# Splitting the weights of the attention pairs three chunks ahead, and moving the scores and their exchange, in a two-layer attention and mLSTM kernel

## The chip, the cores and the metric

The kernel runs on one core of one Trainium2 chip. The time of a run is the device time of one execution in microseconds (us). Three runs of the kernel before took 1404.33, 1407.17 and 1409.06 us; the median is 1407.17 us. Beside the times there is a profile of one execution. Its engines are TensorE (PE, with PEld for its weight loads), VectorE (DVE), ScalarE (ACT), GpSimd (POOL) and SyncE (SP), which only issues transfers here.

## The reference

Two layers over 512 tokens of width 1024, in fp32. Layer 0 has a mixer of dilated attention, layer 1 a chunkwise mLSTM; each is followed by a SwiGLU network of inner width 2816, and all have RMS norms and residual sums. The change concerns the attention, which is, cut to what matters:

```python
DIL_CONFIGS = ((128, 1), (512, 4), (2048, 16))      # window, dilation: three groups
def dilated_attention_mixer(xn, positions, w_in, w_out):
    proj = (xn @ w_in).reshape(B, S, 3, 3, 8, 128)   # group, q/k/v, head, head width
    for g, (window, dilation) in enumerate(DIL_CONFIGS):
        q = apply_partial_rope(proj[:, :, g, 0], positions) * 128 ** -0.5
        k = apply_partial_rope(proj[:, :, g, 1], positions)
        v = proj[:, :, g, 2]
        o, lse = dilated_window_attention(q, k, v, window, dilation)
        outs.append(o); lses.append(lse)
    wts = jax.nn.softmax(jnp.stack(lses), axis=0)
    o = jnp.einsum('gbsh,gbshd->bshd', wts, jnp.stack(outs))
    return o.reshape(B, S, 1024) @ w_out
```

The rope turns only the first 32 of a head's 128 values. The weights of the groups come from the groups' softmax sums, so that all scores of a head are wanted before its probabilities can be weighed and applied to the values.

## The kernel before

**Products.** To keep fp32 accuracy on TensorE each operand is held as a high and a low part, and a product is three matmuls (high-high, high-low, low-high; `SPLITS`). A weight chunk of 128 x 1024 is loaded by SP (`load_chunk`, three places, tag "wraw"); ScalarE copies it to the high part (L210, tile names ending in _h) and VectorE subtracts to get the low part (L211, names in _l). High and low parts have three places each (tags "whi", "wlo", `W_BUFS` = 3). A split into a place has to wait until TensorE has read the chunk that lay there before.

**Pairs.** The eight heads are worked in four pairs, a0 to a3. For each pair there are q and k of three groups. Group 0 is a plain product: two chunks for q and two for k (`project`, L241, names a1g0q, a1g0k), each chunk 48 / 2 = 24 matmuls of 512 columns, for the two heads m = 0 and 1. Groups 1 and 2 are done by `qk_unit` (L904) as seven products of combined blocks, in the order P1, P5, P2, P6, P7, P3, P4 of 24 matmuls of 256 columns. Blocks of weights are combined by VectorE (`less`, L834) and then split as above (names a1g1P_h, a1g2P_l). The products go to three accumulators in PSUM (names ending in c, u, p; tag "acc", three banks). After some products ScalarE copies an accumulator out: L867 after P1, L870 after P5, L872 after P6 (whose copy P7 waits for, since it goes on in the same bank), L861 and L879 after P2 and P4; VectorE combines the parts of k (L885). The rope's steps are on VectorE (L585 to L594), and its copies back on ScalarE (L600 for group 0, eight copies; L602 for the others).

**Attention of a pair.** While TensorE does the projections of pair n, the attention of pair n - 1 is woven in. Its steps are: scores of group 0 (L678 on PE; eight masked reductions L684 on DVE; eight exponentials L715 on ACT), scores of groups 1 and 2 (L698; L701; sixteen exponentials L721), the exchange of maxima and sums and the groups' weights (`joint`, L734 on PE, small steps to L758), weighing of the first and second head (`weigh`, L766 and L769 on DVE), transposes (L775 on DVE, then four transfers of POOL to memory, L778), `bring` (L783, a transfer of POOL back), and the values (L793 and L798 on PE, names a0o). Scores use the PSUM banks of tag "s" for the first head and "o" for the second, two each; the values use "o" too. Probabilities and transposes have the tag "p" with three places, what is brought back has "pt" with two.

**What sets the order.** A chunk or a product ends with a tick (`advance`). Steps are put off by a number of ticks (`defer`): `SCORES0_AT`, `RUN_AT` (scores of groups 1 and 2; the five steps of the rest; the values; the loads of v) and `LAST_AT` for the last pair. The matmuls of such steps are kept at their place on PE by `run` and `fenced`. Weights are split by a plan: `Feed` hands out a chunk and then prepares as many as its `ahead` says (2). Beyond that a scheduler at build time decides the order on every engine; on the chip each engine goes through its own list in that order.

Of the kernel before, what the change touches and what calls it, by code (L numbers as in the profile page):

```python
# [11 lines left out]
F32 = mybir.dt.float32  # L12
# [5 lines left out]
P = 128  # L18
# [3 lines left out]
KC = D // P  # L22
TB = SEQ // P
HEADS = 8
D_FF = 2816
# [8 lines left out]
C3 = float(np.float32(TWO_PI - C1 - C2))  # L34
SCORES0_AT = 4
RUN_AT = (2, (4, 5, 6, 7, 8), (10, 11), (2, 3, 1))
LAST_AT = (1, (3, 3, 3, 3, 3), (), (1, 1, 1))
# [35 lines left out]
def tile_hybrid_dilated_attn_mlstm(  # L73
# [21 lines left out]
    nc.sync.dma_start(cst[:, :K_MT], consts[:, :K_MT])  # L95
    attn_rows = cp.tile([KC, P], F32, name="attn_rows")
    nc.gpsimd.dma_start(attn_rows, attn_norm.rearrange("a (r p) -> (a r) p", p=P))
    ones = cp.tile([P, 1], F32, name="ones")
# [42 lines left out]
    def defer(n, fn):  # L141
        later.append((tick[0] + n, next(order), fn))
# [21 lines left out]
    def last_on_pe():  # L164
        return last_on(mybir.EngineType.PE)
# [32 lines left out]
    def load_chunk(src, shape, name):  # L198
# [4 lines left out]
        return raw, n, view, name  # L203

    def split_chunk(chunk):

        raw, n, view, name = chunk
        hi = wp.tile([P, 1024], F32R, tag="whi", name=name + "_h", bufs=W_BUFS)
        lo = wp.tile([P, 1024], F32R, tag="wlo", name=name + "_l", bufs=W_BUFS)
        nc.scalar.activation(hi[:, :n], raw[:, :n], AF.Copy)  # L210
        nc.vector.tensor_tensor(lo[:, :n], raw[:, :n], hi[:, :n].bitcast(F32), op=ALU.subtract)  # L211
        return view(hi), view(lo)
# [32 lines left out]

    def project(pairs, w2d, c0, nk, evac, name, hook=None, ready=()):

        acc = [acc_tile("%s_%d" % (name, m)) for m in range(2)]
        for ch in range((nk + 3) // 4):
            n = min(4, nk - 4 * ch)  # L250
            whl = ready.pop(0) if ready else split_chunk(weight_chunk(w2d, ch, c0, n, "%s_k%d" % (name, ch)))
            for m in range(2):
                with fenced():
                    multiply(acc[m], whl, pairs, ch, m, nk)
                if 4 * ch + n == nk and hook is None:
                    evac(m, acc[m])
            if 4 * ch + n == nk and hook is not None:
                hook()
                for m in range(2):
                    evac(m, acc[m])  # L260
            advance()
# [122 lines left out]
    with ExitStack() as actx:  # L384
# [54 lines left out]


        xtok = ap.tile([P, TB, D], F32, tag="heads", name="x_tok")
        raws = [wp.tile([P, 1024], F32, tag="wraw", name="first%d_w" % i, bufs=W_BUFS) for i in range(2)]
# [189 lines left out]
        def attention_pair(pr, qks):  # L632
# [33 lines left out]
            def score_bank(i, name):  # L666
                return ps.tile([P, 512], F32, tag="so"[i], name=name, bufs=2)
# [23 lines left out]
            def scores12(qk1, qk2):  # L691

                for i in range(2):
                    for g, (q, k) in ((1, qk1), (2, qk2)):
                        sp = score_bank(i, "%ss%d" % (nm, g))
                        for c in range(4):
                            sl = slice(c * P, (c + 1) * P)
                            nc.tensor.matmul(sp[:, sl], q[:, i, sl], k[:, i, sl], start=True, stop=True)  # L698
                        for c in range(4):
                            sl = slice(c * P, (c + 1) * P)  # L700
                            nc.vector.tensor_tensor_reduce(  # L701
                                p12[i][:, 4 * (g - 1) + c, :], sp[:, sl], mask_causal if g == 1 else mask_dil,
                                1.0, -3e38, op0=ALU.add, op1=ALU.max, accum_out=mx[:, g - 1, i, c:c + 1])
                    exponentials(1, i)

# [65 lines left out]
            def transposes(i):  # L771


                t = ap2.tile([P, 4, 15, R], F32, tag="p", name=nm + "pB", bufs=3)
                nc.vector.transpose(t.rearrange("p b n i -> p n b i"), p[i])  # L775
                d = pts[i] = dp.tile([4, R, 4, 15 * R], F32, tag="d", name=nm + "pD", bufs=2)
                for a in range(4):
                    nc.gpsimd.dma_start(d.rearrange("b j a x -> a j b x")[a],  # L778
                                        t[R * a:R * (a + 1)].rearrange("p b n i -> p b (n i)"))

            def bring(i, queue=nc.gpsimd):
                pt = ap2.tile([P, 4, 15, R], F32, tag="pt", name=nm + "pT", bufs=2)
                queue.dma_start(pt.rearrange("p a n i -> p (a n i)"), pts[i].rearrange("b j a x -> (b j) (a x)"))  # L783
                pts[i] = pt
# [67 lines left out]
        def qk_unit(pr, g, qk):  # L852
# [38 lines left out]
            for n, name in enumerate(ORDER):  # L891
# [16 lines left out]
                if n == 6 and not last:  # L908
                    defer(1, rope(qk, rot, False))
                if n in (1, 3, 5, 6):  # L910
                    advance()

        def project_pair(pr, qks, then=None):
            nm = "a%d" % pr
            for g in range(3):
# [14 lines left out]
                for part in range(2):  # L930
# [58 lines left out]

        HALF = SEQ // 2  # L990
        S = {}
# [302 lines left out]


    HALF = SEQ // 2

# [1021 lines left out]
```

## Time and profile before

| what | value |
|---|---|
| runs | 1404.33, 1407.17, 1409.06 us |
| profiled execution | 1408.34 us, span 1406.6 us |
| TensorE busy | 1375.8 us |
| VectorE busy | 1104.5 us |
| ScalarE busy | 802.5 us |
| GpSimd busy | 163.8 us |
| mean granted clock of TensorE | 0.994 |

The span is the time from the first to the last instruction of the profiled execution; the execution's own time is 1.7 us longer. A row of the waits says which line of which engine waited, for whom, how long in total, how often, and the longest. A row of a timeline has the start, the duration, engine, line, operation, the tile written and those read; brackets at its end give the idle time before it and what ended it. Names have their buffer numbers left out, so that a1g2P_h is the high part of any product of group 2 of pair 1. The attention of the pairs 0 to 2 lies beside the projections of the pairs 1 to 3, between about 177 and 430 us; the last pair's attention follows.

### The profile page before, as it was taken

The page shows a single profiled execution, that of the slowest core. Times are in us where ns is not written, and L with a number is a line of the kernel's source. Part 1 is how long each engine was busy: PE and PEld are TensorE (multiplying, and loading weights), DVE is VectorE, ACT ScalarE, POOL GpSimd, SP SyncE. Part 2 cuts the span into 40 slices and gives each one's busy share as a digit, 9 for nine tenths or more (in the row PEclk, how much of TensorE's full clock was granted, in tenths as well). Part 3 has the DMA queues.
Part 4 walks back from the last instruction along what each step waited for, and adds up shares of the span by engine and source line. Part 5 has one row for each costly group of instructions (what it writes and reads, how often), then busy time and mean ns, then how long its engine had stood idle before and what let it go on. Part 6 is the DMA issues. An engine that isn't in the chain of part 4 may idle for free. (4 is left out here: it accounts for less than half of the span.)

```text
span 1406.6 us, 22635 instructions
## 1 busy us (share of the span) xinstructions
PE 1375.8 (98%) x8740; PEld 1248.3 (89%) x8740; DVE 1104.5 (79%) x1841; ACT 802.5 (57%) x1346; POOL 163.8 (12%) x238
## 2 busy tenths in 40 slices
PE   9999998999989999999999999999999999999997
PEld 7888888988888788999999998888888899999886
DVE  7768668485777289878878888988858987887887
ACT  6556566565755155544466554786534544448854
POOL 3000011111010101000000101113101240001213
PEclk9999999999999999999999999999999999999999
DMA  9534245546165546432354652333333563335963
GB/s 293 171 120 135 93 133 181 171 138 196 49 225 181 187 125 162 133 121 72 109 167 93 146 151 70 97 91 98 98 120 108 127 209 121 119 95 137 197 163 106
DMA packets 140003, 193.67 MB, mean 138 GB/s; under 512 B 8948, under 2 KB 104756, under 8 KB 139896
## 3 DMA queue, kind: packets, MB, share of 16 engines
q1 hardware_dynamic: 119552, 139.81, 31.3%
q0 software_dynamic: 18688, 51.30, 15.6%
q8 instruction: 68, 1.11, 0.3%
q10 hardware_dynamic: 1656, 1.12, 0.2%
q14 instruction: 39, 0.32, 0.1%
HBM read 167.30 MB, written 22.54 MB: 135 GB/s over the span
## 5 line engine op out<-in xcount | busy, mean ns | idle before, releaser
L1622 POOL DMA_DIRECT2D f1T<-in_ffn_w_out_dram x15 | 17.8, 1185 | 208.3 <-DMA f1P_2w_w<-in_ffn_w_out_dram 136.1
L1597 POOL DMA_DIRECT2D f0S<-in_ffn_w_out_dram x10 | 8.7, 890 | 259.5 <-DVE f0hid L1514 173.4
L2154 POOL DMA_DIRECT2D hD<-hB x32 | 21.7, 697 | 67.2 <-DVE hB L2151 67.2
L241 PE MATMUL mo<-n_h,mo_k_l 128*128 128x512 f32 x64 | 25.3, 396 | 0.0
L241 PE MATMUL mo<-n_h,mo_k_h 128*128 128x512 f32 x64 | 25.2, 394 | 0.0
L241 PE MATMUL mo<-n_l,mo_k_h 128*128 128x512 f32 x64 | 25.2, 394 | 0.0
L241 PE MATMUL mwo<-yo_l,mwo_k_h 128*128 128x512 f32 x64 | 25.1, 393 | 0.0
L241 PE MATMUL mqk<-n_h,mqk_k_h 128*128 128x512 f32 x64 | 25.1, 393 | 0.0
L241 PE MATMUL mqk<-n_l,mqk_k_h 128*128 128x512 f32 x64 | 25.1, 392 | 0.0
L241 PE MATMUL awo<-ao_h,awo_k_h 128*128 128x512 f32 x64 | 25.1, 392 | 0.0
L241 PE MATMUL f0j<-n_h,f0j_h 128*128 128x512 f32 x64 | 25.0, 391 | 0.0
L241 PE MATMUL f1j<-n_h,f1j_h 128*128 128x512 f32 x64 | 25.0, 391 | 0.0
L241 PE MATMUL mwo<-yo_h,mwo_k_l 128*128 128x512 f32 x64 | 25.0, 391 | 0.0
L241 PE MATMUL mqk<-n_h,mqk_k_l 128*128 128x512 f32 x64 | 25.0, 391 | 0.0
L241 PE MATMUL f0j<-n_h,f0j_l 128*128 128x512 f32 x64 | 24.9, 390 | 0.0
L241 PE MATMUL f1j<-n_h,f1j_l 128*128 128x512 f32 x64 | 24.9, 390 | 0.0
L241 PE MATMUL awo<-ao_h,awo_k_l 128*128 128x512 f32 x64 | 24.9, 390 | 0.0
L241 PE MATMUL awo<-ao_l,awo_k_h 128*128 128x512 f32 x64 | 24.9, 389 | 0.0
L241 PE MATMUL f0j<-n_l,f0j_h 128*128 128x512 f32 x64 | 24.9, 389 | 0.0
L241 PE MATMUL f1j<-n_l,f1j_h 128*128 128x512 f32 x64 | 24.9, 389 | 0.0
L241 PE MATMUL mwo<-yo_h,mwo_k_h 128*128 128x512 f32 x64 | 24.8, 391 | 0.0
L211 DVE TENSOR_TENSOR v1P_l<-v1W,v1P_h 128x1024 fp32r<-128x1024 f32 x14 | 17.1, 1224 | 9.3 <-ACT v1P_h L210 9.3
(2615 smaller groups left out, 5899.1 us busy)
## 6 DMA issues: line engine op xcount, KB each, us to landing
f0j_w<-in_ffn_w_in_dram SPq DMA_DIRECT2D x17, 512.0 KB, 5.3
f1j_w<-in_ffn_w_in_dram SPq DMA_DIRECT2D x17, 512.0 KB, 6.0
f1T<-in_ffn_w_out_dram POOLq DMA_DIRECT2D x15, 512.0 KB, 6.5
f0hid<-in_ffn_w_in_dram SPq DMA_DIRECT2D x9, 512.0 KB, 5.1
f1hid<-in_ffn_w_in_dram SPq DMA_DIRECT2D x9, 512.0 KB, 5.0
v0W<-in_attn_w_in_dram SPq DMA_DIRECT2D x8, 512.0 KB, 5.8
v1W<-in_attn_w_in_dram SPq DMA_DIRECT2D x8, 512.0 KB, 4.1
awo_k_w<-in_attn_w_out_dram SPq DMA_DIRECT2D x8, 512.0 KB, 4.9
```

The costliest lines, as they stand in the source:

```text
L211: nc.vector.tensor_tensor(lo[:, :n], raw[:, :n], hi[:, :n].bitcast(F32), op=ALU.subtract)
L241: nc.tensor.matmul(acc, whl[a][:, k, m * P:(m + 1) * P], pairs[b][kk], start=(kk == 0 and (a, b) == SPLITS[0]), stop=(kk == nk - 1 and (a, ...
L1597: nc.gpsimd.dma_start(t, src[1][:, ks], accum_op=ALU.add)
L1622: nc.gpsimd.dma_start(view(to), weight_rows(hk * UNITS + u, n), accum_op=ALU.add)
L2154: nc.gpsimd.dma_start(hD[k // 4].rearrange("(b i) x -> i b x", i=R)[:, :, c0:c0 + R], t[R * a_:R * (a_ + 1)])
```

## The change

The line numbers after are 3 to 15 higher in this part (L678 becomes L686, L684 L692, L715 L726, L793 L804, L798 L809, L904 L915, L210 L213, L211 L214).

- The plan prepares three chunks ahead (`feed.ahead = 3`) from the end of the values of all heads until the output projection, and every fourth split goes to a fourth place for high and low part in another pool. The raw weights keep their three places.
- `SCORES0_AT` goes from 4 to 5, so that the scores of group 0 stand one tick later, and `RUN_AT[0]` from 2 to 1: the scores of groups 1 and 2 stand after the first chunk of g0q of the next pair and no longer after the second. All their matmuls come first, then the reductions by head.
- With `amid`, steps that are due at the next tick (exchange, joint, first weighing) run within the last chunk of g0k, between its two heads, 12 matmuls sooner.
- Probabilities, transposes and what is brought back share one tag with four places (before: three and two). The first `bring` stands after the second transposes, so that on POOL's queue eight transfers to memory come ahead of both transfers back.
- The rope's copies of group 2 follow its steps at once and are not put off by a tick.
- The rope's tables are filled by half as wide copies on POOL and one transfer more for each table, and a few tiles lie in other pools.

```diff
-SCORES0_AT = 4
-RUN_AT = (2, (4, 5, 6, 7, 8), (10, 11), (2, 3, 1))
+SCORES0_AT = 5
+RUN_AT = (1, (4, 5, 6, 7, 8), (10, 11), (2, 3, 1))
...
+    spare = []
+    splits = itertools.count()
+
     def split_chunk(chunk):
         raw, n, view, name = chunk
-        hi = wp.tile([P, 1024], F32R, tag="whi", name=name + "_h", bufs=W_BUFS)
-        lo = wp.tile([P, 1024], F32R, tag="wlo", name=name + "_l", bufs=W_BUFS)
+        p, more, bufs = (spare[0], "4", 1) if spare and next(splits) % (W_BUFS + 1) == W_BUFS else (wp, "", W_BUFS)
+        hi = p.tile([P, 1024], F32R, tag="whi" + more, name=name + "_h", bufs=bufs)
+        lo = p.tile([P, 1024], F32R, tag="wlo" + more, name=name + "_l", bufs=bufs)
...
                 if 4 * ch + n == nk and hook is None:
                     evac(m, acc[m])
+                if amid and (ch, m) == (1, 0):
+                    with tc.issue_after(last_on_pe()):
+                        run_deferred(lambda t: t <= tick[0] + 1)
...
-                    nc.gpsimd.tensor_copy(
-                        to[R * (c // 2):R * (c // 2 + 1)].rearrange("p (m s) -> p m s", m=2)[:, :, c % 2 * P:(c % 2 + 1) * P],
-                        t[R * c:R * (c + 1)].unsqueeze(1).to_broadcast([R, 2, P]))
+                    nc.gpsimd.tensor_copy(to[R * (c // 2):R * (c // 2 + 1), c % 2 * P:(c % 2 + 1) * P],
+                                          t[R * c:R * (c + 1)])
+                nc.gpsimd.dma_start(to[:2 * R, HALF:], to[:2 * R, :HALF])
                 nc.gpsimd.dma_start(to[2 * R:], to[:2 * R])
...
-                p.extend(ap2.tile([P, 15, P], F32, tag="p", name="%sp%d" % (nm, i), bufs=3) for i in range(2))
+                p.extend(ap2.tile([P, 15, P], F32, tag="p", name="%sp%d" % (nm, i), bufs=4) for i in range(2))
...
-                for i in range(2):
-                    for g, (q, k) in ((1, qk1), (2, qk2)):
-                        sp = score_bank(i, "%ss%d" % (nm, g))
+                banks_ = {}
+                for g, (q, k) in ((1, qk1), (2, qk2)):
+                    for i in range(2):
+                        sp = banks_[g, i] = score_bank(i, "%ss%d" % (nm, g))
...
+                for g, i in ((1, 0), (2, 0), (1, 1), (2, 1)):
+                    for c in range(4):
+                        nc.vector.tensor_tensor_reduce(
...
+                    if g == 2:
+                        exponentials(1, i)
...
-                t = ap2.tile([P, 4, 15, R], F32, tag="p", name=nm + "pB", bufs=3)
+                t = ap2.tile([P, 4, 15, R], F32, tag="p", name=nm + "pB", bufs=4)
...
-                pt = ap2.tile([P, 4, 15, R], F32, tag="pt", name=nm + "pT", bufs=2)
+                pt = ap2.tile([P, 4, 15, R], F32, tag="p", name=nm + "pT", bufs=4)
...
-            rest = (first_rest, lambda: transposes(0), lambda: (bring(0), weigh(1)), lambda: transposes(1),
+            rest = (first_rest, lambda: transposes(0), lambda: weigh(1), lambda: (transposes(1), bring(0)),
                     lambda: bring(1))
...
                 if n == 6 and not last:
-                    defer(1, rope(qk, rot, False))
+                    back = rope(qk, rot, False)
+                    if g == 2:
+                        back()
+                    else:
+                        defer(1, back)
...
-                        project(pair, w_in, base + part * D, KC, evac, "%sg%d%s" % (nm, g, "qk"[part]), ready=feed)
+                        project(pair, w_in, base + part * D, KC, evac, "%sg%d%s" % (nm, g, "qk"[part]), ready=feed,
+                                amid=pr > 0 and part == 1)
...
         ap2 = pool(actx, "attn2")
+        spare.append(ap2)
+        feed.ahead = 3
...
+        spare.clear()
```

On VectorE, where the weights of group 2 of pair 1 are split, there stands before (p5 in a name is an accumulator, a1s a bank of scores, a1nb the negated maxima; the last four L211 are the low parts of P6, P7, P3 and P4):

```order
L684 ISA a1p_2071,a1own<-a1s_2087,acst 128x256
L684 ISA a1own 128x1
L710 TENSOR_SCALAR a1nb<-a1own 128x4
L211 TENSOR_TENSOR a1g2P_l<-a1g2W_1966,a1g2P_h 128x1024
L710 TENSOR_SCALAR a1nb<-a1own 128x4
L834 TENSOR_TENSOR a1g2W_1892<-a1g2W_1968,a1g2W_1892 128x1024
L834 TENSOR_TENSOR a1g2W_1966<-a1g2W_1966,a1g2W_1892 128x1024
L211 TENSOR_TENSOR a1g2P_l<-a1g2W_1892,a1g2P_h 128x1024
L211 TENSOR_TENSOR a1g2P_l<-a1g2W_1894,a1g2P_h 128x1024
L211 TENSOR_TENSOR a1g2P_l<-a1g2W_1968,a1g2P_h 128x1024
L211 TENSOR_TENSOR a1g2P_l<-a1g2W_1966,a1g2P_h 128x1024
```

On the same engine at the same place there stands after (the first four L214 are the low parts of P6, P7, P3 and P4; a2g0q is the first chunk of pair 2):

```order
L214 TENSOR_TENSOR a1g2P_l<-a1g2W_1853,a1g2P_h 128x1024
L214 TENSOR_TENSOR a1g2P_l<-a1g2W_1855,a1g2P_h 128x1024
L845 TENSOR_TENSOR a1g2W_1933<-a1g2W_1933,a1g2W_1853 128x1024
L214 TENSOR_TENSOR a1g2P_l<-a1g2W_1935,a1g2P_h 128x1024
L214 TENSOR_TENSOR a1g2P_l<-a1g2W_1933,a1g2P_h 128x1024
L214 TENSOR_TENSOR a2g0q_k_l<-a2g0q_k_w,a2g0q_k_h 128x1024
L692 ISA a1p_2147,a1own<-a1s_2149,acst 128x128
L692 ISA a1own 128x1
L692 ISA a1p_2147,a1own<-a1s_2149,acst 128x256
L692 ISA a1own 128x1
L692 ISA a1p_2147,a1own<-a1s_2154,acst 128x256
```

The reductions of the scores stood ahead of the splits of P2 and P6; now they stand behind all splits of the group and behind that of the next pair's first chunk.

On ScalarE at the same place there stands before (L715 are the exponentials of the scores of group 0; the three L210 are the high parts of P6, P7 and P3):

```order
L867 ACTIVATE a1g2u<-a1g2c_2108 128x512
L715 ACTIVATE a1p_2070,a1own<-a1p_2070,a1nb 128x128
L715 ACTIVATE a1p_2070,a1own<-a1p_2070,a1nb 128x256 x3
L715 ACTIVATE a1p_2071,a1own<-a1p_2071,a1nb 128x128
L715 ACTIVATE a1p_2071,a1own<-a1p_2071,a1nb 128x256 x3
L210 ACTIVATE a1g2P_h<-a1g2W_1892 128x1024
L870 ACTIVATE a1g2vu<-a1g2p_2139 128x512
L210 ACTIVATE a1g2P_h<-a1g2W_1894 128x1024
L861 ACTIVATE rot<-a1g2c_2108 32x512
L879 ACTIVATE a1g_q<-a1g2c_2108 128x2x256
L210 ACTIVATE a1g2P_h<-a1g2W_1968 128x1024
```

And after, from the high part of P3 on:

```order
L213 ACTIVATE a1g2P_h<-a1g2W_1935 128x1024
L213 ACTIVATE a1g2P_h<-a1g2W_1933 128x1024
L872 ACTIVATE rot<-a1g2c_2082 32x512
L890 ACTIVATE a1g_q<-a1g2c_2082 128x2x256
L213 ACTIVATE a2g0q_k_h<-a2g0q_k_w 128x1024
L883 ACTIVATE a1g2vu<-a1g2u 128x512
L726 ACTIVATE a1p_2147,a1own<-a1p_2147,a1nb 128x128
L726 ACTIVATE a1p_2147,a1own<-a1p_2147,a1nb 128x256 x3
L726 ACTIVATE a1p_2148,a1own<-a1p_2148,a1nb 128x128
L726 ACTIVATE a1p_2148,a1own<-a1p_2148,a1nb 128x256 x3
```

The exponentials stood ahead of P6's high part; now they stand behind all splits of the group and the copy of P6's result.

More of the change, by code (lines that the diff above doesn't have):

```diff
@@ L23 @@
 TB = SEQ // P
+HALF = SEQ // 2
 HEADS = 8
@@ L95, in tile_hybrid_dilated_attn_mlstm @@
     nc.sync.dma_start(cst[:, :K_MT], consts[:, :K_MT])
-    attn_rows = cp.tile([KC, P], F32, name="attn_rows")
-    nc.gpsimd.dma_start(attn_rows, attn_norm.rearrange("a (r p) -> (a r) p", p=P))
     ones = cp.tile([P, 1], F32, name="ones")
@@ L244, in multiply, with project @@
                     stop=(kk == nk - 1 and (a, b) == SPLITS[-1]))
-    def project(pairs, w2d, c0, nk, evac, name, hook=None, ready=()):
+    def project(pairs, w2d, c0, nk, evac, name, hook=None, ready=(), amid=False):
         acc = [acc_tile("%s_%d" % (name, m)) for m in range(2)]
@@ L438, in tok_tile @@
             return ap.tile([P, 2, SEQ], F32, tag="qk", name=name, bufs=6)
+        attn_rows = vp.tile([KC, P], F32, name="attn_rows")
+        nc.gpsimd.dma_start(attn_rows, attn_norm.rearrange("a (r p) -> (a r) p", p=P))
         xtok = ap.tile([P, TB, D], F32, tag="heads", name="x_tok")
@@ L698, in scores12 @@
                             nc.tensor.matmul(sp[:, sl], q[:, i, sl], k[:, i, sl], start=True, stop=True)
[L699 to L704, printed above, removed]
+                for g, i in ((1, 0), (2, 0), (1, 1), (2, 1)):
+                    for c in range(4):
+                        nc.vector.tensor_tensor_reduce(
+                            p12[i][:, 4 * (g - 1) + c, :], banks_[g, i][:, c * P:(c + 1) * P],
+                            mask_causal if g == 1 else mask_dil,
+                            1.0, -3e38, op0=ALU.add, op1=ALU.max, accum_out=mx[:, g - 1, i, c:c + 1])
+                    if g == 2:
+                        exponentials(1, i)
             def exponentials(o, i):
@@ L988, in renew @@
                 nc.vector.tensor_tensor(pair[1][k], src, pair[0][k].bitcast(F32), op=ALU.subtract)
-        HALF = SEQ // 2
         S = {}
@@ L1293, in norm @@
         return pair, rbc, r, hook
-    HALF = SEQ // 2
     PRODUCTS = (("A11", "B11"), ("S1", "T1"), ("S2", "T2"), ("A12", "B21"), ("S3", "T3"), ("S4", "B22"), ("A22", "T4"))
```

## The prediction

> **What bounds the kernel now.** I read the page first, then TensorE's waits in the part of the kernel that the change touches, then the granted clock around each wait, and last the order of the work that ends each wait on ScalarE and VectorE.
>
> ```profile
> span 1406.6 us, 22635 instructions
> PE 1375.8 (98%) x8740; PEld 1248.3 (89%) x8740; DVE 1104.5 (79%) x1841; ACT 802.5 (57%) x1346; POOL 163.8 (12%) x238
> ```
>
> TensorE is busy 98% of the span, and the change leaves its number of matmuls as it is. It can only gain time in which TensorE waits or runs at a lower clock, or add to that time. The waits of TensorE by what it waited for, in three windows, one for each of the pairs 1, 2 and 3 (names a1, a2, a3; total, times, longest):
>
> ```profile
> PE a1g2u L904 <- ACT a1g2P_h L210: 1.4, 1, 1.4
> PE a1g1p L904 <- ACT a1g1P_h L210: 1.1, 1, 1.1
> PE a1g1p L904 <- DVE a1g1P_l L211: 0.9, 1, 0.9
> PE a1g2u L904 <- DVE a1g2P_l L211: 0.8, 1, 0.8
> ...
> PE a2g2u L904 <- ACT a2g2P_h L210: 1.7, 1, 1.7
> PE a2g1p L904 <- ACT a2g1P_h L210: 1.1, 1, 1.1
> PE a2g1p L904 <- DVE a2g1P_l L211: 0.9, 1, 0.9
> PE a2g2u L904 <- DVE a2g2P_l L211: 0.8, 1, 0.8
> PE a2g2c L904 <- ACT a2g2u L867: 0.2, 1, 0.2
> ...
> PE a3g2u L904 <- ACT a3g2P_h L210: 1.7, 1, 1.7
> PE a3g2c L904 <- ACT a3g2u L867: 1.3, 1, 1.3
> PE a3g1p L904 <- ACT a3g1P_h L210: 1.1, 1, 1.1
> PE a3g1p L904 <- DVE a3g1P_l L211: 0.9, 1, 0.9
> PE a3g2u L904 <- DVE a3g2P_l L211: 0.8, 1, 0.8
> ```
>
> Every pair has the same two places. Place A is the wait for the split of product P3 of group 1 (rows g1p): 2.0 us in each pair. Place B is the wait for the split of P6 of group 2 (rows g2u, with the copy g2u L867): 2.2, 2.7 and 3.8 us. Together 14.7 us. The clock around the waits (stretch, length, then busy time of PE, PEld, DVE, ACT, POOL, then the granted clock):
>
> ```profile
> 219.00:223.00 4.00, 3.54 (x17) 3.54 (x18) 4.00 (x10) 0.48 (x1) 0.64 (x2) 0.60 0.94 205
> 243.00:247.00 4.00, 3.24 (x16) 3.07 (x15) 3.12 (x3) 2.94 (x5) 0.00 (x0) 0.58 0.45 137
> 323.00:328.00 5.00, 2.57 (x20) 2.16 (x19) 2.48 (x3) 5.00 (x14) 0.00 (x0) 1.00 0.03 12
> 410.00:414.00 4.00, 4.00 (x23) 4.00 (x23) 3.64 (x5) 1.98 (x4) 0.00 (x0) 0.61 0.40 122
> ```
>
> After three of the six places (A and B of pair 1, B of pair 3) the clock falls for some 4 us, which loses (1 - 0.60) x 4 = 1.6, then 1.7 and 1.6 us: 4.9 us. After B of pair 2 it stays at 1.00, and it does so at the two places that aren't shown. So 14.7 + 4.9 = 19.6 us is all that these places can give back, 1.4% of the span.
>
> What ends the waits, from the rows of pair 1 on ScalarE, VectorE and TensorE (start, duration):
>
> ```profile
> 213.61 1.46 ACT L600 ACTIVATE a1g_k<-rot 32x256 f32<-32x256 f32 x4
> 217.01 1.99 ACT L210 ACTIVATE a1g1P_h<-a1g1W 128x1024 fp32r<-128x1024 f32 x2
> 218.91 0.57 ACT L872 ACTIVATE a1g1vu<-a1g1u 128x512 f32<-128x512 f32 x1
> 241.58 1.04 ACT L210 ACTIVATE a1g2P_h<-a1g2W 128x1024 fp32r<-128x1024 f32 x1
> ...
> 211.00 0.63 DVE L594 TENSOR_TENSOR rot<-rot 128x512 f32<-128x512 f32 x1
> 235.00 0.42 DVE L684 CUSTOM_DVE_ANT_0 a1p<-a1s,acst 128x256 f32<-128x256 f32 x1
> 235.34 0.29 DVE L684 CUSTOM_DVE_ANT_0 a1p<-a1s,acst 128x128 f32<-128x128 f32 x1
> 235.56 0.42 DVE L684 CUSTOM_DVE_ANT_0 a1p<-a1s,acst 128x256 f32<-128x256 f32 x1
> 242.65 1.22 DVE L211 TENSOR_TENSOR a1g2P_l<-a1g2W,a1g2P_h 128x1024 fp32r<-128x1024 f32 x1 [2.31 <-ACT a1g2P_h L210]
> ...
> 218.10 0.39 PE L904 MATMUL a1g1p<-S4h,a1g1P_h 128*128 128x256 f32 x1 [1.12 <-ACT a1g1P_h L210]
> ```
>
> At B the eight exponentials of the scores (L715) stand on ScalarE ahead of P6's high half, which begins at 241.58; the low half follows at 242.65 and takes 1.22. At A TensorE stands from 216.98 (218.10 less 1.12); the rope copies (L600), two copies out of an accumulator (L861, L879) and two splits stand ahead of the copy L872, for which P7 waits. Prices from here: high to low half 1.07 us start to start, a reduction L684 0.34 (256 wide) or 0.22 (128 wide) start to start, a rope step 0.63, a copy out of an accumulator 0.57.
>
> **The change part by part.** Place B. In the order of the changed kernel all splits of group 2 stand on ScalarE ahead of the exponentials, so P6 finds its weights ready; what covers them is the work ahead of it, 72 matmuls of P1, P5 and P2 and the scores. I take the whole of it: -(2.2 + 2.7 + 3.8) = -8.7 us. If half the cover failed it would be -4.
>
> What is late next. The scores of group 0 (L678) now lie between P5 and P2, not ahead of P1, so their eight reductions come later; and on VectorE they stand behind the splits that run three chunks ahead. Two matmul products (P2, P6) later come the values of the previous pair's first head (L793), which need the bank that the scores of this pair fill until its reductions are done. Before there was no wait there:
>
> ```profile
> 237.75 0.28 PE L904 MATMUL a1g2p<-S,a1g2P_l 128*128 128x256 f32 x1
> 238.11 0.28 PE L904 MATMUL a1g2p<-S,a1g2P_l 128*128 128x256 f32 x1
> ...
> 248.03 0.50 PE L793 MATMUL a0o<-a0pT,a0v 128*128 128x128 f32 x3
> ```
>
> In pair 1 the low half of a2g0q_k0 stands ahead of the reductions. With four places its high half takes the place of the chunk four before it, P6, so it cannot begin before P6's last matmul, the very one after which the values want to run. From there: 0.1 for the release, 1.07 high half, 1.22 low half, four reductions of the first head (0.22 + 3 x 0.34 = 1.24), two of the second (0.56), 0.1 for the release: 4.3 us, all of it on the path. In pairs 2 and 3 the last split ahead of them is P4's, which takes P2's place: the same 4.3 from P2's end, less P6's own 24 matmuls (0.36 us for three by the rows of P5, so 2.9): 1.4 us. In pair 3 three rope steps of 0.63 stand between as well: 3.3 us. Sum +9.0 us. Bounds: 4.3, if only pair 1 shows it, and 15, if the load of the chunk lands late as well (rival 2). I take 9.0, since each piece has its row.
>
> Place A. The weighing of the first head's probabilities comes sooner (the exchange runs 12 matmuls, 2.7 us, ahead), but on VectorE it now stands ahead of the rope's last step, which in pair 1 ended at 211.6 and will end near 214.6 (3 us is my estimate: it now follows the eight weighings, some 2 us, and a split that waits for P1's end). From there eight rope copies (2 x 1.46), one split (1.04), two copies (1.14) and the copy that P7 needs (0.57) end at 220.3. TensorE gets there at 218.7 (216.98, 1.0 later by the next part, six matmuls of P3 ahead of P7 at 0.12): 1.6 us. In pairs 2 and 3 the weighing comes ahead of P6's low half, and the order has 14 matmuls of P3 ahead of P7: a split and the copy after P6's end, 0.1 + 1.04 + 0.57 + 0.1, less 14 x 0.12 = 1.7, leave 0.1, and 0.8 if the weighing is late by as much as in pair 1; I take 0.5 each. So 2.6 instead of 6.0: -3.4 us, between -6 and 0.
>
> Scores of groups 1 and 2 a chunk sooner. Their 16 exponentials and a split of group 1 stand ahead of the copies of g0q on ScalarE, and g0k's second accumulator takes the bank that the first of these free (TensorE's g0q and scores, then ScalarE):
>
> ```profile
> 179.52 0.58 PE L241 MATMUL a1g0q<-xa_h,a1g0q_k_h 128*128 128x512 f32 x1
> 190.64 3.74 PE L698 MATMUL a0s<-a0g_k,a0g_q 128*128 128x128 f32 x32
> ...
> 190.44 0.74 ACT L944 ACTIVATE rot<-a1g0q 32x256 f32<-32x256 f32 x2
> 191.19 0.60 ACT L946 ACTIVATE a1g_q<-a1g0q 128x512 f32<-128x512 f32 x1
> 194.22 0.40 ACT L721 ACTIVATE a0p<-a0p,a0nb 128x128 f32<-128x128 f32 x1 [0.23 <-DVE a0nb L710]
> ```
>
> The exponentials begin about when the scores' 32 matmuls end (194.22 against 190.64 + 3.74). 16 x 0.40 + 1.04 + 0.74 + 0.60 = 8.8 us later the bank is free. TensorE wants it after 24 + 12 matmuls, each (190.64 - 179.52)/48 = 0.23 us, 8.3 us after the scores; with another 0.5 for the second head's exponentials, which wait for reductions, I take +1.0 us in pair 1, and nothing in the others, whose order has the split of group 1 behind these copies (1.04 less). The rope copies of the previous pair's group 2 can be some 0.2 us late for their scores in pairs 2 and 3, an estimate. Sum +1.4, between 0 and +3.
>
> The clock. Of the six places with waits of 2.0 to 3.8 us three were followed by a fall worth 1.6. Now two long waits are left (4.3, 3.3) and shorter ones. By the trace's one in two, the two long ones and A of pair 1 would bring 1.5 falls, 2.4 us, and a sum 0.8 us lower; I count two, 3.2 instead of 4.9, since the long ones are longer than half of those that fell: -1.7 us, between -4.9 and +3. The Trainium skill ("TensorE: Matmul & The Clock Gate", the table under "Why this matters for your kernels") asks for no gap over about 3 us between bursts. The trace differs: falls after 2.0 and 2.2 us. By that rule the two long waits alone would bring a fall, which is my count.
>
> At nothing: the rope tables' copies and their new transfer (first used long after they land, and TensorE waits for nothing before pair 1); the shared places of probabilities and transposes, whose transfers to memory were done when the next scores came; the first bring behind the second transposes, on POOL's queue, whose 8 + 2 transfers stay the same; the weights of the output projection one chunk sooner, where the only wait is for the last pair's transposes, which do not move. If that cover goes, each is worth one late transfer in a pair.
>
> Sum: -8.7 + 9.0 - 3.4 + 1.4 - 1.7 = -3.4 us. The profiled run took 1408.34 us (span 1406.6 and 1.7 around it) and becomes 1404.9; it lies 1.2 above the median of the runs, 1407.17, so the median becomes about 1403.8.
>
> **The rivals.** (1) *More is covered.* The head start of 2.7 us covers A and the bank wait wholly, and pairs 2 and 3 have no wait for the values: another -2.6 - 1.4 - 4.7 us and one fall less (-1.6) give 1393.5, and the half of it 1398.6. For it: VectorE is idle 2.31 us ahead of P6's low half, so there is room. Against: P6's place is released where I said, however idle the engines are.
>
> (2) *Slower: the load of the chunk split ahead.* There are still three places for raw weights, so a split three chunks ahead stands in VectorE's queue for a load that can start only when an older raw place is free, and the reductions stand behind it. The transfers of this stretch (KB each, median us to landing):
>
> ```profile
> a1g2W<-in_attn_w_in_dram SPq DMA_DIRECT2D x3, 512.0 KB, 6.8
> a2g0q_k_w<-in_attn_w_in_dram SPq DMA_DIRECT2D x2, 512.0 KB, 4.7
> ```
>
> By my chain the load just lands ahead of P6's end at 4.7 us. At 6.8 the wait grows by 2.1 in each of three pairs, and one or two more falls of the clock come with it: +6.3 + 1.6 to 3.2, so 1412 to 1413. It decides from about 1.3 us of lateness in each pair.
>
> (3) *No gain, the waits only move.* B turns into the wait for the values (-8.7 and +9.0 are that already), A stays at 2 us, and the clock falls as often: 1407 to 1408.
>
> **How the numbers follow.** My forecast, 1403.8, has 0.42, with a range of its own from 1400 to 1407; 0.18 of it lies below the bound of 0.3%, 4.2 us under 1407.17, which is about what a measurement of this kernel can tell from no change. Rival 1 has 0.25 (faster), rival 2 0.22 (slower), rival 3 0.08; what is left, 0.03, is for mishaps that I don't see (slower). Faster 0.25 + 0.18 = 0.43; the same 0.24 + 0.08 = 0.32; slower 0.25. For 8 times in 10 the range takes in the better part of rival 1, down to 1395, and of rival 2, up to 1412.5.
>
> **What would show it.** In the profile after: no wait for P6's split at L915 in any pair; a wait of a0o at L804, about 4.3 us, released by VectorE's L692 or by the split a2g0q_k0; smaller ones of a1o and a2o; A with 1.6 us in pair 1 and under 1 in the others; a wait of a1g0k for a bank, 1 us. The forecast is wrong if the wait of a0o is missing (then rival 1), or if the releaser there is a transfer (rival 2), or if P6 still waits.

## The result and the profile after

The changed kernel takes 1407.91 us (median of 20 runs, 1405.57 to 1409.38) against 1407.01 us before (20 runs, 1404.33 to 1409.67): a ratio of 1.0005, 95% interval 0.9998 to 1.0011. That is no change that this measurement can tell. The profiled execution took 1408.62 us (span 1406.8) against 1408.34 (1406.6).

The waits of TensorE in the profile after, in four windows: pairs 1, 2, 3, and the last pair's own attention (total, times, longest):

```profile
PE a0o L804 <- DVE a1own L692: 4.1, 1, 4.1
PE a1g1u L915 <- ACT a1g1vu L883: 1.5, 1, 1.5
PE a1g0k L244 <- ACT a1g_q L961: 0.9, 1, 0.9
...
PE a1o L804 <- DVE a2own L692: 1.2, 1, 1.2
PE a2g1u L915 <- ACT a2g1vu L883: 0.9, 1, 0.9
...
PE a2o L804 <- DVE a3own L692: 3.2, 1, 3.2
PE a3g1u L915 <- ACT a3g1vu L883: 1.1, 1, 1.1
...
PE a3o L804 <- DMA a3pT<-a3pD: 2.5, 1, 2.5
```

Place B is gone in all three pairs. In its stead the values (a0o, a1o, a2o) wait for the reductions of the scores: 8.5 us, where B had 8.7. A, now a wait for the copy L883, is 3.5 instead of 6.0. The bank of g0k costs 0.9. In the pairs that makes 12.9 us of waits instead of 14.7.

What ends the longest of them, on ScalarE, VectorE and TensorE (start, duration):

```profile
243.42 1.06 ACT L213 ACTIVATE a2g0q_k_h<-a2g0q_k_w 128x1024 fp32r<-128x1024 f32 x1 [0.86 <-PE a1g2u L915]
...
244.50 1.23 DVE L214 TENSOR_TENSOR a2g0q_k_l<-a2g0q_k_w,a2g0q_k_h 128x1024 fp32r<-128x1024 f32 x1 [1.65 <-ACT a2g0q_k_h L213]
245.65 0.28 DVE L692 CUSTOM_DVE_ANT_0 a1p<-a1s,acst 128x128 f32<-128x128 f32 x1
...
247.59 0.80 PE L804 MATMUL a0o<-a0pT,a0v 128*128 128x128 f32 x2 [4.09 <-DVE a1own L692]
```

The high half of the next pair's first chunk begins when P6's last matmul has released its place, the low half follows, then the reductions, and then the values. The chain is the one of the forecast, step by step.

The clock (stretch, length, busy time of PE, PEld, DVE, ACT, POOL, then the granted clock), in stretches that are set to the points where the clock changes, or to whole periods of it (the last section says which):

```profile
242.35:245.77 3.42, 1.15 (x10) 0.94 (x8) 1.77 (x3) 1.75 (x3) 0.00 (x0) 1.00 0.90 280
245.77:249.18 3.41, 1.59 (x7) 1.60 (x8) 2.65 (x18) 0.84 (x4) 0.00 (x0) 0.50 0.56 177
249.18:252.59 3.41, 3.41 (x18) 3.41 (x17) 0.00 (x0) 2.98 (x14) 0.00 (x0) 0.50 0.03 9
...
409.61:413.02 3.41, 3.12 (x14) 3.12 (x15) 2.81 (x10) 2.37 (x11) 0.00 (x0) 0.50 0.81 289
...
471.05:474.46 3.41, 0.88 (x5) 0.42 (x3) 0.19 (x1) 0.00 (x0) 0.00 (x0) 1.00 0.90 337
474.46:477.87 3.41, 3.41 (x16) 3.41 (x17) 0.00 (x0) 0.00 (x0) 0.00 (x0) 0.50 0.77 297
```

There are falls to half clock behind the waits of 4.1 and 3.2 us, and each loses half of TensorE's busy time in it. The first is a long one, 6.83 us, and loses (1.59 + 3.41) / 2 = 2.5 us. The second loses 3.12 / 2 = 1.6. A third fall, 3.41 / 2 = 1.7 us, stands behind the wait for the last pair's transposes (2.5 us). In the profile before, that wait was 2.4 us and the clock stayed at 1.00:

```profile
PE a3o L793 <- DMA a3pT<-a3pD: 2.4, 1, 2.4
...
472.34:475.76 3.42, 1.89 (x9) 1.23 (x7) 1.23 (x1) 0.04 (x1) 0.00 (x0) 1.00 0.80 287
475.76:479.17 3.41, 2.59 (x23) 2.62 (x24) 0.00 (x0) 0.00 (x0) 0.00 (x0) 1.00 0.97 377
```

A has no fall any more. Together the falls cost 5.8 us. Counted in the same way the three falls before cost 5.0 us (3.41, 3.14 and 3.41 us of busy time at half clock); the prediction's 4.9 was read from stretches of 4 us.

### The profile page after: what moved, and what is told of

It reads as the page before. It is cut to its first block, busy times and chain, and to the rows that moved or that the text cites. A ratio compares the mean times of both kernels' runs of the same rounds, so it can differ in the third digit from the quotient of the medians.

```text
span 1406.8 us, 22647 instructions
## 1 busy us (share of the span) xinstructions
PE 1377.5 (98%) x8740; PEld 1249.7 (89%) x8740; DVE 1105.8 (79%) x1841; ACT 803.7 (57%) x1346; POOL 163.1 (12%) x240
## 5 line engine op out<-in xcount | busy, mean ns | idle before, releaser
L214 DVE TENSOR_TENSOR v1P_l<-v1W,v1P_h 128x1024 fp32r<-128x1024 f32 x14 | 17.1, 1223 | 9.3 <-ACT v1P_h L213 9.3
```

## The experiments

The first four ran together (before: 1407.1 us there, 7 runs), the last four as well (before: 1408.09 us, 21 runs). The kernel before was thus 1.1 us slower there than beside the changed kernel (1407.01), so for the last four the ratio says more than the time. Names are those of the expectations.

**reductions_first.** An order for the scheduler, without a semaphore on the chip (`reduced` holds the last reduction of `scores0`, three times; `order` stands for the call that adds a dependency for the build alone):

```diff
         nc.vector.tensor_tensor(lo[:, :n], raw[:, :n], hi[:, :n].bitcast(F32), op=ALU.subtract)
+        if reduced:
+            order(last_on(DVE), reduced.pop())
```

> The changed kernel, with the eight reductions of the scores of group 0 ordered on VectorE ahead of the next three splits' low halves (P3, P4 and the next pair's first chunk), by an order without a semaphore; all else stays. Theory of the queue: the waits of the values (4.1, 1.2 and 3.2 us in the profile after) are made by the splits that stand ahead of the reductions, so they go, and with them the two falls of the clock that followed them (about 2.5 and 1.6 us). That gives -8.5 -4 = -12 us against the changed kernel, 1395 to 1397; the waits for the copy L883 (1.5, 0.9, 1.1) and for the bank (0.9) stay. Rival, lateness is passed on: P3 and P4, now split 2.5 us later, make TensorE wait instead, at most 2.5 us in each pair, and the time stays above 1403. Rival, the time of these waits isn't what the kernel's time hangs on (the last pair's transposes come at a fixed time): 1405 to 1408.

Measured: 1398.41 us, ratio 0.9941 (0.9926 to 0.9956), 9.5 us less than the changed kernel. Its waits for the values and at A, over all three pairs:

```profile
PE a1g1u L922 <- ACT a1g1vu L890: 1.5, 1, 1.5
...
PE a2g1u L922 <- ACT a2g1vu L890: 1.0, 1, 1.0
...
PE a2o L811 <- DVE a3own L697: 2.5, 1, 2.5
PE a3g1u L922 <- ACT a3g1vu L890: 1.1, 1, 1.1
```

The waits of a0o and a1o are gone, and nothing took their place. That of a2o shrank to 2.5 only: in pair 3 three rope steps stayed ahead of the reductions, which the edit didn't touch. This one wait, with the fall of 1.7 us that the profile has behind it, is more than the 1.4 us that the run lacks to the expected 1395 to 1397. The two rivals fall.

**scores0_later_alone.** The kernel before, with one number:

```diff
-SCORES0_AT = 4
+SCORES0_AT = 5
```

> The kernel before with one number changed, the scores of group 0 one tick later (after P5 instead of ahead of P1). By the built order the reductions come behind P6's low half and the exponentials behind P7's high half, so P6 no longer waits for its split. Theory of the queue: place B (2.2, 2.7, 3.8 us) goes, no wait for the values takes its place since the reductions stand ahead of P7, P3 and P4, place A (2.0 each) stays; two of three falls go too (1.7 each): -8.7 -3.4 = -12 us, about 1395. Rival, the values wait for the later scores anyway (they have only P2 and P6 for their reductions): a wait of 1 to 4 us in each pair, and 1400 to 1407.

Measured: 1396.46 us, ratio 0.9931 (0.9914 to 0.9948). In the pairs only A is left:

```profile
PE a1g1p L904 <- ACT a1g1P_h L210: 1.1, 1, 1.1
PE a1g1p L904 <- DVE a1g1P_l L211: 0.9, 1, 0.9
...
PE a2g1p L904 <- ACT a2g1P_h L210: 1.1, 1, 1.1
PE a2g1p L904 <- DVE a2g1P_l L211: 0.8, 1, 0.8
...
PE a3g1p L904 <- ACT a3g1P_h L210: 1.1, 1, 1.1
PE a3g1p L904 <- DVE a3g1P_l L211: 0.9, 1, 0.9
```

So the scores, as late as in the changed kernel, do not make the values wait. One fall of the clock is left in this profile, behind A of pair 3. One line of the change is worth 10.6 us, and the rest of the change took it back.

**scores0_later_shared_places.** The same, and the shared places:

```diff
-SCORES0_AT = 4
+SCORES0_AT = 5
...
-                p.extend(ap2.tile([P, 15, P], F32, tag="p", name="%sp%d" % (nm, i), bufs=3) for i in range(2))
+                p.extend(ap2.tile([P, 15, P], F32, tag="p", name="%sp%d" % (nm, i), bufs=4) for i in range(2))
...
-                t = ap2.tile([P, 4, 15, R], F32, tag="p", name=nm + "pB", bufs=3)
+                t = ap2.tile([P, 4, 15, R], F32, tag="p", name=nm + "pB", bufs=4)
...
-                pt = ap2.tile([P, 4, 15, R], F32, tag="pt", name=nm + "pT", bufs=2)
+                pt = ap2.tile([P, 4, 15, R], F32, tag="p", name=nm + "pT", bufs=4)
...
-            rest = (first_rest, lambda: transposes(0), lambda: (bring(0), weigh(1)), lambda: transposes(1),
+            rest = (first_rest, lambda: transposes(0), lambda: weigh(1), lambda: (transposes(1), bring(0)),
```

> The kernel before with the scores of group 0 one tick later and the probabilities, transposes and what is brought back in four shared places (with the first bring behind the second transposes), nothing else. By the built order the shared places put the reductions behind the low half of P4, which with three weight places waits for P6's last matmul. Theory of the queue: B goes (-8.7), but the values wait about 4.3 us in the pairs 1 and 2 and 5 in pair 3 (+13.5), with three falls of the clock at them: 1410 to 1414. Rival, the sharing itself costs nothing and the order on VectorE doesn't matter: the same time as the run without sharing, about 1395.

Measured: 1415.75 us, ratio 1.0068 (1.0053 to 1.0083), 19.3 us more than without the sharing. The new waits:

```profile
PE a0o L793 <- DVE a1own L684: 4.1, 1, 4.1
...
PE a1o L793 <- DVE a2own L684: 4.1, 1, 4.1
...
PE a2o L793 <- DVE a3own L684: 4.3, 1, 4.3
PE a3g2p L904 <- DVE a3g2P_l L211: 1.1, 1, 1.1
```

They sum to 13.6 us, and the falls of the clock lose 6.8 us in this profile (two of them last 6.83 us) against 1.6 without the sharing: 18.8 us more together.

The sharing moves little work. It changes what a reduction has to wait for. With shared places the first head's reductions wait for the transfers of the previous pair's first transposes, and the second head's for those of the second; with separate places the first head's wait for none and the second head's for those of the first. In the order that the scheduler then builds, the reductions stand behind the splits of P7, P3 and P4, and with separate places ahead of them. No row of these profiles has a reduction of the pairs 1 to 3 waiting for a transfer; what holds them is the place in VectorE's list. That the place in the list makes the waits is shown by this run and the first; that the transfers are what moved them in the list is read from the two built programs and not tried by itself, and neither is the place of the first `bring`, which moved along.

**no_fourth_no_shared.** The changed kernel without these two parts:

```diff
-        spare.append(ap2)
-        feed.ahead = 3
...
-                p.extend(ap2.tile([P, 15, P], F32, tag="p", name="%sp%d" % (nm, i), bufs=4) for i in range(2))
+                p.extend(ap2.tile([P, 15, P], F32, tag="p", name="%sp%d" % (nm, i), bufs=3) for i in range(2))
...
-                t = ap2.tile([P, 4, 15, R], F32, tag="p", name=nm + "pB", bufs=4)
+                t = ap2.tile([P, 4, 15, R], F32, tag="p", name=nm + "pB", bufs=3)
...
-                pt = ap2.tile([P, 4, 15, R], F32, tag="p", name=nm + "pT", bufs=4)
+                pt = ap2.tile([P, 4, 15, R], F32, tag="pt", name=nm + "pT", bufs=2)
```

> The changed kernel without the fourth place (two chunks ahead, three places) and without the shared places (three for probabilities and transposes, two for what is brought back); the scores and the exchange stay moved, so do the rope's copies and tables. By the built order the reductions stand behind P6's low half, ahead of P7, P3 and P4. Theory of the queue: no wait for the values and no place B; at A the copy that P7 waits for comes right after P4's high half, about 1.0 us of wait in pair 1 and 0.3 to 0.6 in the others; the bank's wait of 0.9 stays. About 3 us of waits instead of 14.7 before, and no falls of the clock: -11.7 -5 = -16.7 us, 1390 to 1393. Rival, splitting three chunks ahead was needed: P6 or P3 wait for their splits again, 3 to 9 us, and the time is 1398 to 1405.

Measured: 1396.21 us, ratio 0.9925 (0.9910 to 0.9940). The waits in pair 2, to which those of pair 3 are equal and those of pair 1 add 0.5 for the bank:

```profile
PE a2g1p L915 <- DVE a2g1P_l L214: 0.9, 1, 0.9
PE a2g1u L915 <- DVE a2g1P_l L214: 0.5, 1, 0.5
PE a2g1u L915 <- ACT a2g1vu L883: 0.2, 1, 0.2
```

No B and no wait for the values, as expected, and the clock stays at 1.00 in all three pairs. The time is 3 us above the expected range: at A, P6 and P3 wait for their low halves, which stand behind the weighing and the transposes; I had seen only the copy's wait. These waits sum to 5.3 us and not to 3. The rival, that splitting three ahead was needed, is right by that much and no more.

**waits_filled.** Matmuls that nobody reads, where TensorE stood:

```diff
         def values(i, out=None):
+            for j in range({0: 16, 2: 12}.get(pr, 0) if i == 0 else 0):
+                nc.tensor.matmul(idle_bank, pair[0][j % KC][:, :P], pair[0][j % KC], start=True, stop=True)
```

> The changed kernel with matmuls that nobody reads (16 in pair 1, 12 in pair 3, 128x512 into a bank that is free there) on TensorE just ahead of the values, where it stood 4.1 and 3.2 us. They take about 3.6 and 2.7 us, so that the values start when they did. Theory of the clock: the falls there (2.5 and 1.6 us in the profile after) come of standing still, so they go, and the time is 1403 to 1405 (-3 to -4). Rival: the falls come of something else in these stretches: the same time as the changed kernel, 1407 to 1408.

Measured: 1402.75 us, ratio 0.9962 (0.9949 to 0.9976), 5.2 us less than the changed kernel (6 us by the two ratios), with 28 matmuls more; that is a little below the expected range. The values start as late as before (247.50 against 247.59), and the clock does not fall:

```profile
PE a0o L809 <- DVE a1own L692: 0.4, 1, 0.4
...
PE a2o L809 <- DVE a3own L692: 0.4, 1, 0.4
```

```profile
247.00:251.00 4.00, 3.56 (x32) 3.50 (x32) 1.34 (x10) 2.75 (x12) 0.00 (x0) 1.00 0.42 129
251.00:255.00 4.00, 4.00 (x36) 4.00 (x35) 0.69 (x1) 2.62 (x9) 0.55 (x1) 1.00 0.17 66
```

So the falls come of standing still. The two falls that the matmuls took away had cost 2.5 + 1.6 us. The profile has no fall at the last pair's transposes either (a wait of 2.3 us), where the profile after lost 1.7 us; nothing was put there.

**scores_not_sooner.** The changed kernel, with the scores of groups 1 and 2 and the exchange at their old places:

```diff
-RUN_AT = (1, (4, 5, 6, 7, 8), (10, 11), (2, 3, 1))
+RUN_AT = (2, (4, 5, 6, 7, 8), (10, 11), (2, 3, 1))
...
-                                amid=pr > 0 and part == 1)
+                                amid=False)
```

> The changed kernel with the scores of groups 1 and 2 back at their old place (after the second chunk of g0q) and the exchange after the whole of g0k; all else stays. My forecast gave this part -3.4 at place A and +1.4 at the bank. By the built order without it the rope's copies come ahead of the weighing and ScalarE's chain to the copy ends at about 219.4 when 13 matmuls of P3 are done, so A would be near 1.1 us in each pair, and the bank's wait is gone; the waits for the values stay. Theory that the gain at A was the fourth place's and not the move's: 1406 to 1408, no slower than the changed kernel. Rival, the move gave it: A returns to 2.0 us in each pair, 1409 to 1411.

Measured: 1409.52 us, ratio 1.0011 (1.0002 to 1.0020), where the changed kernel has 1.0005 (0.9998 to 1.0011). The time lies in the rival's range, but the intervals overlap, so it doesn't decide between the theory and the rival. The waits do:

```profile
PE a0o L804 <- DVE a1own L692: 4.9, 1, 4.9
PE a1g1p L915 <- DVE a1g1P_l L214: 1.1, 1, 1.1
PE a1g2p L915 <- ACT a1g_q L890: 0.6, 1, 0.6
...
PE a2g1u L915 <- ACT a2g1vu L883: 0.5, 1, 0.5
PE a2g1u L915 <- DVE a2g_k L896: 0.3, 1, 0.3
PE a2g1p L915 <- DVE a2g1P_l L214: 0.2, 1, 0.2
...
PE a2o L804 <- DVE a3own L692: 4.3, 1, 4.3
```

A did not return to 2.0: it is 1.1 in pair 1 and about 1.0 in pair 2, with all its rows. The gain at A thus doesn't need the move. What grew are the waits for the values, by 0.8 and 1.1 us; that the kernel as a whole is slower without the move isn't shown.

**all_reordered and all_reordered_three_places.** Two orders: all splits and rope steps on VectorE behind the reductions, and on ScalarE the copy of P6's result ahead of the rope's copies and of the next group's first split. Once in the changed kernel, once with three weight places and separate places for the probabilities. (`copied` holds the copy of P6's result, `backs` the rope's copies of group 0.)

```diff
         nc.scalar.activation(hi[:, :n], raw[:, :n], AF.Copy)
+        if copied:
+            order(last_on(ACT), copied[0])
         nc.vector.tensor_tensor(lo[:, :n], raw[:, :n], hi[:, :n].bitcast(F32), op=ALU.subtract)
+        if reduced:
+            order(last_on(DVE), reduced[0])
...
             nc.vector.stream_shuffle(sh, a, shift)
+            if reduced:
+                order(last_on(DVE), reduced[0])
...
                     nc.scalar.activation(vu[:, 1], acc["u"], AF.Copy)
+                    copied[:] = [last_on(ACT)]
+                    if g == 1:
+                        while backs:
+                            order(backs.pop(), copied[0])
```

> The changed kernel with two orders added, neither with a semaphore: on VectorE the eight reductions of the scores of group 0 come ahead of every later split and rope step, also in pair 3; on ScalarE the copy of P6's result in group 1 comes ahead of the rope's eight copies and of the next group's first split. Theory of the queue: of the waits of reductions_first the one for the values in pair 3 (2.5 us, and the fall of 1.6 behind it) and the three for the copy (1.5, 1.0, 1.1) go, the bank's 0.6 stays: -7.7 us against that run's 1398.4, 1389 to 1392. Rival: the copies put off make the next product wait (the bank of its accumulator is freed 4 to 5 us later), 1 to 2 us in each pair: 1394 to 1397.

Measured: 1393.16 us, ratio 0.9892 (0.9879 to 0.9906), the fastest of all, between the expected range and that of the rival. In the pairs 1.1 us of waits are left:

```profile
PE a1g0k L251 <- ACT a1g_q L978: 0.5, 1, 0.5
PE a1g2c L932 <- DVE a1g2P_l L219: 0.2, 1, 0.2
PE a1g1u L932 <- DVE a1g_k L913: 0.2, 1, 0.2
...
PE a3g1u L932 <- DVE a3g_k L913: 0.2, 1, 0.2
```

The waits of 1 to 2 us in each pair that the rival named are not there. The profile has one fall of 1.7 us, behind the last pair's wait (2.2 us), where that of reductions_first had none.

> The same two orders, with the three weight places, two chunks ahead, and separate places for probabilities (as in no_fourth_no_shared). Theory of the queue: P6's wait of 0.5 stays in each pair, P7's becomes about 0.4, P3's 0.9 goes, the bank's 0.5 stays: about 3.2 us of waits, 1393 to 1395. So the fourth place is worth 2 to 4 us once the reductions are out of its way. Rival: the fourth place is worth nothing even then: the same time as all_reordered within 1 us.

Measured: 1413.82 us, ratio 1.0033 (1.0022 to 1.0044). My expectation was 20 us too low. P5 of group 2 waits for its split, by 3.2, 2.7 and 3.4 us, with a fall of the clock in each pair:

```profile
PE a1g2p L932 <- DVE a1g2P_l L219: 3.2, 1, 3.2
...
PE a2g2p L932 <- DVE a2g2P_l L219: 2.7, 1, 2.7
...
PE a3g2p L932 <- DVE a3g2P_l L219: 3.4, 1, 3.4
```

VectorE's rows of pair 1 say why:

```profile
224.51 1.18 DVE L219 TENSOR_TENSOR a1g1P_l<-a1g1W,a1g1P_h 128x1024 fp32r<-128x1024 f32 x1
...
233.16 1.22 DVE L858 TENSOR_TENSOR a1g2W<-a1g2W,a1g2W 128x1024 f32<-128x1024 f32 x1 [4.00 <-DMA a1g2W<-in_attn_w_in_dram]
```

With three places P4's high half must wait for P6's end, where it now also stands behind the eight rope copies; its low half (224.51) so comes late, a raw weight place stays taken, and the load that the next combination of blocks needs lands 4 us too late. With four places P4 is split ahead of the copies. So under these orders the fourth weight place together with the shared places beats three weight places with separate ones by 20.7 us. The same orders cost the kernel with three weight places about 16 us (no_fourth_no_shared took 10.9 us less than the kernel before beside it, this run 5.7 more). Without the order on ScalarE the three places were ahead: no_fourth_no_shared took 2.2 us less than reductions_first. What the fourth place of the weights is worth without the sharing stays open.

## Why the prediction was right, and where not

The forecast was a small gain to 1403.8 us, and of all cases together faster had 0.43 and the same 0.32. Measured is the same: 1407.91 us lies 4.1 us above the forecast and inside the wide range of 1395 to 1412.5, but outside the forecast's own (1400 to 1407) and in that of rival (3), which had 0.08. The mechanism was right; the term of the sum that failed is the clock's. By its own steps:

- *Place B, -8.7:* right. No row of it is left in the profile after, and the move of the scores alone takes it away too.
- *The wait for the values, +9.0:* right in place, releaser and size: 4.1, 1.2 and 3.2 against 4.3, 1.4 and 3.3. Two runs confirm the mechanism from opposite sides: the reductions put ahead take it away (in pair 3 only the wider orders of all_reordered do), the shared places bring it to the kernel before with nothing else but the later scores.
- *Place A, -3.4:* right in kind, 0.9 too large. A is 1.5, 0.9 and 1.1 against 1.6, 0.5 and 0.5. For the pairs 2 and 3 I had taken 0.5 between a count that gave 0.1 and a bound of 0.8; the bound was nearer. The sooner exchange, from which I worked it out, isn't needed: with the exchange at its old place A is as short (3.1 us in all). With the sooner exchange and without the fourth place it is 4.8 (no_fourth_no_shared).
- *The bank and the copies, +1.4:* 0.9 at the bank, nothing at the copies, which I had as 0.2 in two pairs.
- *The sum of the waits in the pairs:* -8.7 + 9.0 - 3.4 + 1.4 = -1.7 forecast; 12.9 - 14.7 = -1.8 measured. Here the errors cancel, -0.5, +0.9 and -0.5; that is luck.
- *The clock, -1.7:* this step failed. From the trace's one in two I counted two falls of 1.6 where before had three. The fall behind 4.1 us lost 2.5, since it began while TensorE still stood and lasted twice as long, and a third came at a place that I had costed at nothing because its wait does not move: the last pair's transposes. In all 5.8 us instead of 5.0, so +0.8 instead of -1.7. I had taken the length of a wait to decide; the last section shows what does. All the runs together agree that the clock gave nothing back: its mean is 0.9942 over the 20 runs after and 0.9950 over the 21 of the kernel before beside the last four experiments. These means include the end of the span, where TensorE has nothing left to do.
- *At nothing:* right for the waits (the last pair's is 2.5 against 2.4, and nothing else shows), wrong for the clock there.

Waits (-1.8 and +0.1) and clock (+0.8) together give -0.9 us for the profiled execution, whose span grew by 0.2. The same matmuls found in both profiles show where the rest lies. The changed kernel is 0.2 us late when the first scores start (176.84 against 176.67). It gains 2.8 us in the pairs (first matmul of a3g12v at 426.80 against 429.38), 1.8 of it in waits and 0.9 in clock. It loses 2.3 us in the last pair's attention and the output projection (first matmul of f0j at 507.61 against 507.90), 1.8 of it by the wait and the fall. After that it wins 0.15 and has 0.7 us more behind the last matmul, which the forecast didn't look at. So in the pairs, where all terms of the forecast lay, 2.8 of its 3.4 us came about in this execution, and they were lost after the pairs. Single executions of one kernel differ by 4 to 5 us. The forecast for the median was made against the profiled execution of before, less 1.2 us.

Of the rivals, *more is covered* falls for this kernel, since P6's place was released where I said. *Slower by the load* falls too: the releaser of a0o is L692, and no wait of TensorE in the pairs ends with a transfer; that a late split holds a raw place and makes a load late showed only under other orders (all_reordered_three_places). *The waits only move* has the time right, but it left A at 2 us, while A shortened; the falls were as many as it said and cost 0.8 us more.

## What to carry to other kernels

Where several small moves are made together, time each by itself: one number was worth 10.6 us here, and the shared places took back more than that. A buffer that is shared adds a wait to whoever writes it next. Even where that wait is over in time on the chip, it can change the order that a scheduler builds (so the built programs read; it wasn't tried by itself), and an engine that works through its list in order will then hold up others behind work that is not urgent. A short order without a semaphore, put on the few instructions that another engine waits for, took 9.5 us off the changed kernel. Wider orders took more off with four weight places and cost about 16 us with three, so look first for what an order holds back.

## What the runs showed of the hardware

A wait of TensorE costs more than its length once the clock falls. In the profile after TensorE stopped near 243.5 (247.59 less 4.09); the clock is at 1.00 up to 245.77 and at 0.50 from there to 252.59, so that it fell some 2.3 us after the stop and stayed low for about 5 us of work. The wait of 4.1 us cost 6.6.

The falls keep to periods. In the profile after the clock changes at 245.77, 252.59, 409.61, 413.02, 474.46 and 477.87 us, and all of these lie whole multiples of 3.413 us apart. It is so in each of the ten profiles that has a fall ahead of the last matmul, and every such fall lasts 3.41 or 6.83 us. What counts is how long TensorE stands within one period. Over the ten profiles, a period at full clock in which it stood for 1.95 us or more was followed by half clock each time (16 periods), one with 1.6 us or less never, and of six in between three were. A period's place against the kernel's start differs from profile to profile: the first full clock comes 6.83 us after the start in the profile after, and 4.73 us in the one before. That is why waits of 2.4 and 2.5 us at the same place went once without and once with a fall: before, the end of a period at 475.76 cut the wait into 1.5 and 0.8 us of standing (3.42 less 1.89, 3.41 less 2.59); after, all 2.5 us (3.41 less 0.88) lay in one period, which ended at 474.46. Where a period ends in a given execution is luck, and so was the third fall in the profile after.

Matmuls that nobody reads, in the time of the wait, kept the clock at 1.00 there and made the kernel 5.2 us faster, of which the two falls are 4.1, though the values started no sooner.

The Trainium skill ("TensorE: Matmul & The Clock Gate", Part 1) puts the loss of the clock after an idle window of some 3.4 us, and the window as running free of the program. The runs agree with the length and with the running free, as the multiples of 3.41 us show; but the window need not be idle throughout: 1.95 us of standing in it were enough each time, and there the measurement decides.
